# Three sets of slots for Mixer C's masked operands, half a bank per score level, and one buffer per operand part of the out-projection

## The chip, the cores and the metric

The kernel runs on one core of a Trainium2 chip. The metric is the device time of one launch in microseconds (us), and lower is better. TensorE (PE) does the matmuls, VectorE (DVE), ScalarE (ACT) and GpSimd (POOL) the element-wise work, and SyncE (SP) issues most of the DMA transfers. Each engine works through its own instructions in a fixed order and waits on semaphores for the others. Operands lie in the on-chip buffer of 128 partitions, and matmuls write to the accumulator memory, of which the program uses banks of 128 partitions x 2 KB.

## The reference

One layer of a hybrid decoder trunk, for a prompt of 2048 tokens and 64 sample tokens (8 sequences of 8) that share all weights. `x` has 1024 columns; one input projection feeds three mixers, A (gated DeltaNet), B (an RG-LRU) and C (gated linear attention, GLA), and then

```python
x = layer_norm(ALPHA * x + W_out @ [A(x) | B(x) | C(x)])
x = layer_norm(ALPHA * x + ConvFFN(x))            # d_ff = 2816

def gla_chunked(q, k, v, logf, s0):               # mixer C: 6 heads, dk 32, dv 64, chunks of 64 tokens
    # S_t = diag(f_t) S_{t-1} + k_t v_t^T ;  o_t = S_t^T q_t
```

Inside a chunk of 64 tokens, GLA needs the scores of every query with every earlier key, each weighted by the product of the per-channel forget gates between the two; between chunks a state of 32 x 64 per head is carried. Mixer C's output is normalised per head and gated before it enters `W_out`.

## The kernel before

The program has four stages, one after the other with overlaps at the seams: the input projection (to about 540 us), mixers A and B (to about 1000 us), mixer C with the out-projection and the first layer norm (`window_c`, about 985 to 1495 us), and the ConvFFN (`phase3`, to the end, almost nothing but dense matmuls). All matmuls of projections are done in three parts (`mm3`, L320): both operands are split into a high and a low part, and high x high, low x high and high x low are summed.

The change lies in `window_c`. Its work comes in nine groups: the sample group g8 (64 tokens), then g0 to g7 of 256 tokens (4 chunks). A group has 6 heads, so there are 54 heads in all.

Per group, `prep` makes decayed keys and queries (`natural`), transposes values and keys on PE (`tokens`, tiles `pv` and `pk`) and then, head by head, calls `fill` and `scores`. The scores of a chunk are found at three levels of a tree (blocks of 16, 4 and 1 tokens): level l has masked operands K1/Q1, K2/Q2, K3/Q3 of 128 x 256, and these six tiles are one set of slots. `fill` writes a head's set: ACT copies parts of K (L1347, L1355, L1358) and of Q3 (L1360, four), POOL multiplies Q1 and Q2 (L1351, six) and a row block of RC (L1361), and SP issues six DMAs K<-KN (L1349, L1357), of 32 KB each. `scores` multiplies Q by K at each level for four chunks on PE (L1373, four matmuls, eight records in the trace) and reads the result out of the accumulator into RC: ACT copies level 1 (L1376), DVE overwrites by mask with levels 2 and 3 (L1379). Masked places that nothing writes must be zero; they are cleared once, at the start, by a POOL memset of each slot tile. Two sets of slots are used in turn (`h % 2`). Levels 1 and 2 of a head share one bank (`pa`), level 3 lies in another (`pb`), and each name has one buffer per bank.

`chain` steps through a group's chunks: the state update `cs` (L1427), the output `po` (L1430), ACT's copy of the state into the next chunk's XC (L1436), and after every two chunks `head_norm` (a ones-matmul at L1206, ACT and DVE), which writes mixer C's part of `mx`.

`Project`, called P below, is the out-projection of 128 tokens `t0`: 17 calls, for the sample tokens (2048) first and then 0, 128 to 1920. `mh` is the high part of `mx` (ACT, L1524), `ml` the low part (POOL, L1525), then come two halves `pm` of 24 matmuls 128x512 each (48 a call), DVE adds the residual (L1531) and does the layer norm, SP stores `s_x1` (L1536). One call later PE transposes the result (`pt`, L1549, eight), ACT copies it into `xt` (L1550), which has a single buffer, and SP stores `s_x1T` (L1552). `pm` and `pt` share two banks. `spare()` lends the buffers of `mx`, `mh`, `ml` and `xt` to the sample group before P needs them.

The order of `window_c` on each engine is set by the scheduler of the framework, which plans with costs of its own; P is given the lowest priority, so its pieces fill places that the plan sees as free. `phase3` is scheduled by hand. A position below is told by the number of prompt score levels that stand ahead of it on PE: three for each of the 48 heads, 144 in all.

Of the kernel before, what the change touches and what calls it, by code (L numbers as in the profile page):

```python
# [9 lines left out]
F32R = mybir.dt.float32r  # L10
# [11 lines left out]
KD = DM // 128  # L22
# [281 lines left out]
def load_consts(E, pool, names):  # L304
    t = {}
    for n in names:
        o, w = _CST[n]
        t[n] = pool.tile([128, w], F32, name="c_" + n)
        E.nc.sync.dma_start(t[n], E.d["consts"][:, o:o + w])
    return t  # L310


def mm3(nc, ps, wh, wl, xh, xl, first=True, last=True, by_k=False):

    n = len(wh)
    seq = [(wh, xh), (wl, xh), (wh, xl)]
    order = [(a, k) for k in range(n) for a in range(3)] if by_k else [(a, k) for a in range(3) for k in range(n)]
    for i, (a, k) in enumerate(order):
        w, x = seq[a]
        nc.tensor.matmul(ps, w[k], x[k], start=first and i == 0, stop=last and i == 3 * n - 1)  # L320
# [854 lines left out]
def ln_scale(E, mv, m):  # L1175

    E.aset(LNEXP)
    v = mv[:m, ..., 1:2]
    E.nc.scalar.activation(v, v, AF.Ln, bias=EPS)
    E.nc.scalar.activation(v, v, AF.Exp, scale=-0.5)  # L1180
# [32 lines left out]
class Gla:  # L1213
# [4 lines left out]
    def __init__(self, E, ctx):  # L1218
        nc, tc = E.nc, E.tc
        self.E = E  # L1220
        E.aset(LNEXP)
        early = ctx.enter_context(tc.tile_pool(name="ce", bufs=1))
        self.early = ctx.enter_context(tc.tile_pool(name="cf", bufs=2))
        pool = ctx.enter_context(tc.tile_pool(name="c1", bufs=1))
        self.tr = ctx.enter_context(tc.tile_pool(name="c2", bufs=2))
        self.pg = {t: ctx.enter_context(tc.tile_pool(name="c" + t, bufs=1, space=PSUM)) for t in ("s", "tk", "g")}
        self.C = load_consts(E, early, ["m2", "m3", "m2s", "bj", "i32"])

        def ring(name, n, c, w):
            return [pool.tile([128, 6, c, w], F32, name=f"{name}{i}") for i in range(n)]  # L1230

        self.RC, self.XC, self.KC = ring("RC", 2, 4, 64), ring("XC", 2, 4, 64), ring("KC", 2, 4, 32)
        sg = [early.tile([128, 6, 1, 64], F32, name="RCs")], ring("XCs", 1, 1, 64), ring("KCs", 1, 1, 32)
        self.slots = [{n: early.tile([128, 256], F32, name=f"{n}_{i}") for n in ("K1", "Q1", "K2", "Q2", "K3", "Q3")}
                      for i in range(2)]
        self.sls = [{n: early.tile([128, 64], F32, name=f"{n}_s{i}") for n in ("K2", "Q2")} for i in range(2)]

        self.KN = [{l: early.tile([128, 512 >> t], F32, name=f"KN{l}_{t}") for l in (1, 2, 3)} for t in range(2)]

        self.DD = [{l: early.tile([128, n, 6], F32, name=f"D{l}_{i}") for l, n in ((1, 4), (2, 16), (3, 64))}  # L1240
                   for i in range(2)]
        self.ebs = pool.tile([32, 6, 8], F32, name="ebs")
        for r in sg:
            nc.vector.memset(r[0][0:64], 0.0)
        nc.vector.memset(sg[0][0][64:], 0.0)
        for d in self.sls + self.KN + self.slots:
            for w in d.values():
                nc.gpsimd.memset(w, 0.0)
        for d in self.DD:
            for w in d.values():  # L1250
                nc.gpsimd.memset(w, 1.0)
        for w in self.RC + self.XC + self.KC:
            nc.gpsimd.memset(w[0:64], 0.0)
        self.G = []
        for g in range(9):
            o = Env()
            o.g, o.smp, o.t0 = g, g == 8, g * 256
            o.RC, o.XC, o.KC = (r[0] for r in sg) if o.smp else (r[g % 2] for r in (self.RC, self.XC, self.KC))
            o.nch = 1 if o.smp else 4
            o.n = 64 * o.nch  # L1260
            self.G.append(o)
# [69 lines left out]
    def fill(self, g, h):  # L1331

        nc = self.E.nc
        t, r0 = divmod(h, 4)
        r = slice(r0 * 32, r0 * 32 + 32)
        d, n = g.nat[t], g.n
        S = self.slots[h % 2]
        if g.smp:
            sl = self.sls[h % 2]
            for a in (1, 3):  # L1340
                o = slice(32 * a, 32 * a + 32)
                nc.scalar.copy(v4(sl["K2"][o], 4)[:, :, a - 1], v4(d["k2"][r], 4)[:, :, a - 1])
                nc.gpsimd.tensor_tensor(v4(sl["Q2"][o], 4)[:, :, a], v4(d["q"][r], 4)[:, :, a],
                                        v4(d["q2"][r], 4)[:, :, a], op=OP.mult)
        for l, w in (() if g.smp else ((1, 16), (2, 4))):
            kk, qq = d[f"k{l}"][r], d[f"q{l}"][r]
            nc.scalar.copy(v4(S[f"K{l}"][32:64], w)[:, :, 0], v4(kk, w)[:, :, 0])  # L1347
            for i in range(2):
                nc.sync.dma_start(S[f"K{l}"][64 + 32 * i:96 + 32 * i, :n], self.decayed(g, t, l, i)[r])  # L1349
            for a in (1, 2, 3):  # L1350
                nc.gpsimd.tensor_tensor(v4(S[f"Q{l}"][32 * a:32 * a + 32], w)[:, :, a], v4(d["q"][r], w)[:, :, a],  # L1351
                                        v4(qq, w)[:, :, a], op=OP.mult)
        K3, Q3 = S["K3"][:, :n], S["Q3"][:, :n]
        kk, qq = d["k"][r], d["q"][r]
        nc.scalar.copy(v4(K3[0:32], 1)[:, :, 0], v4(kk, 1)[:, :, 0])  # L1355
        for i in range(2):
            nc.sync.dma_start(K3[32 + 32 * i:64 + 32 * i], self.decayed(g, t, 3, i)[r])  # L1357
        nc.scalar.copy(K3[96:128], d["k2"][r])  # L1358
        for a in range(4):
            nc.scalar.copy(v4(Q3[32 * a:32 * a + 32], 1)[:, :, a], v4(qq, 1)[:, :, a])  # L1360
        nc.gpsimd.tensor_tensor(g.RC[0:32, h].rearrange("p c i -> p (c i)"), qq, d["q0"][r], op=OP.mult)  # L1361

    def scores(self, g, h):
        nc, C, m = self.E.nc, self.C, g.nch
        o = g.RC[64:, h].rearrange("p c i -> p (c i)")
        pa = self.psum(f"s{g.g}_{h}", (128, 2, 4, 64))
        pb = self.psum(f"s3{g.g}_{h}", (128, 4, 64))
        for l in (2, 3) if g.smp else (1, 2, 3):
            ps = pb if l == 3 else pa[:, l - 1]
            K, Q = (self.sls[h % 2][x + "2"] if g.smp and l == 2 else self.slots[h % 2][f"{x}{l}"] for x in "KQ")  # L1370
            for c in range(m):
                i = slice(c * 64, (c + 1) * 64)
                nc.tensor.matmul(ps[64:, c], K[:, i], Q[:, i], start=True, stop=True)  # L1373
            a = ps[64:, :m].rearrange("p c i -> p (c i)")
            if l == 1:
                nc.scalar.copy(o, a)  # L1376
            else:
                mk = C["m2s" if g.smp and l == 2 else f"m{l}"][64:, :m * 64]
                nc.vector.copy_predicated(o, mk.bitcast(U32), a)  # L1379
# [92 lines left out]
def v4(a, w):  # L1472
    return a.rearrange("p (n a i) -> p n a i", a=4, i=w)


class Project:
# [21 lines left out]

    def spare(self):

        tags = [("mx", 2), ("mh", 2), ("ml", 2), ("xt", 1)]
        return [self.tr.tile([128, 2, 6, 64], F32, tag=t, bufs=b, name="sp" + t) for t, b in tags]

    def dest(self, t0):
# [13 lines left out]
    def __call__(self, t0):  # L1518
        E, nc = self.E, self.E.nc
        m = min(128, TT - t0)  # L1520
        mx, x = self.M[t0]
        h = self.tr.tile([128, KD, 128], F32R, tag="mh", name=f"mh{t0}")
        lo = self.tr.tile([128, KD, 128], F32R, tag="ml", name=f"ml{t0}")
        nc.scalar.copy(h, mx)  # L1524
        nc.gpsimd.tensor_tensor(lo, mx, h.bitcast(F32), op=OP.subtract)  # L1525
        for j in range(2):
            ps = self.pm.tile([128, 512], F32, tag="pm", name=f"pm{t0}{j}")
            js = slice(j * 512, (j + 1) * 512)
            mm3(nc, ps, [h[:, k] for k in range(KD)], [lo[:, k] for k in range(KD)],
                [self.wh[:, k, js] for k in range(KD)], [self.wl[:, k, js] for k in range(KD)])  # L1530
            nc.vector.scalar_tensor_tensor(x[:m, js], x[:m, js], ALPHA, ps[:m], op0=OP.mult, op1=OP.add)  # L1531
        mv = self.tr.tile([128, 2], F32, tag="mv", bufs=3, name=f"mv{t0}")
        ln_stats(E, x, m, mv, self.tr.tile([128, 2, 6], F32, tag="st", name=f"st{t0}"))
        ln_scale(E, mv, m)
        ln_apply(E, x, m, mv, self.g, self.b)
        nc.sync.dma_start(E.s["x1"][t0:t0 + m], x[:m])  # L1536
        self.done.append((t0, m, x))
# [443 lines left out]
```

## Time and profile before

| | |
|---|---|
| median of the three runs, us | 3026.18 (3017.28 to 3026.94) |
| profiled execution: time, span, us | 3025.96, 3024.2 |
| PE busy | 2886.8 us, 95% |
| DVE, ACT, POOL busy | 50%, 41%, 28% |
| first matmul of P(2048) | 1083.4 us |
| last `pm` matmul of P(1920) | begins before 1493.2 us |
| first dense run of `puv` (ConvFFN) | 1507.7 us |

The span is what the trace shows from the first to the last instruction; the execution's time is 1.8 us longer. Times below are counted from the span's start. PE is busy almost throughout, but busy is not the same as fast: the profile also gives the clock that was granted to PE (PEclk, 1.00 is full), and a matmul at half the clock is busy for longer.

### The profile page before, as it was taken

The numbers are of one execution on the slowest core, as the hardware profiler recorded it, in microseconds if no ns is written. First come the engines' busy times: TensorE is split into PE (matmuls) and PEld (weight loads), VectorE is DVE, ScalarE is ACT, GpSimd is POOL, SyncE is SP. The second block draws the span as 40 slices with busy tenths as digits, with TensorE's granted clock in tenths as the row PEclk, the third lists the DMA queues.
The fourth block names the chain that finished last, engine by engine and source line by source line (L and its number), as shares of the span: only waits on it lengthen the run. The fifth ranks groups of instructions, "written<-read, shape, count | busy, mean of one in ns | idle before, by whom it ended". The sixth has DMA issues, their size and how long they took to land.

```text
span 3024.2 us, 45238 instructions
## 1 busy us (share of the span) xinstructions
PE 2886.8 (95%) x17755; PEld 2490.4 (82%) x17755; DVE 1510.9 (50%) x2454; ACT 1231.4 (41%) x2591; POOL 844.2 (28%) x898
## 2 busy tenths in 40 slices
PE   8999999788889799999899999999999999999998
PEld 7888789777779577767678888888889999999997
DVE  4564443577663676756533333333376443344436
ACT  4474443446653687766332222222232222222223
POOL 0000001734423545444222222222232222222224
PEclk9999999789999579999899999999999999999999
DMA  6221113533433443533531111111134111111111
GB/s 198 83 74 68 58 59 96 144 101 111 114 95 99 108 130 110 150 112 117 180 116 45 46 56 49 51 48 42 49 112 146 42 52 47 48 42 42 49 43 62
DMA packets 196508, 256.77 MB, mean 85 GB/s; under 512 B 43170, under 2 KB 162040, under 8 KB 196232
## 3 DMA queue, kind: packets, MB, share of 16 engines
q1 hardware_dynamic: 194168, 246.58, 26.6%
q0 software_dynamic: 1984, 7.12, 0.6%
q8 instruction: 140, 2.29, 0.3%
q14 instruction: 72, 0.59, 0.1%
q10 hardware_dynamic: 144, 0.20, 0.0%
HBM read 183.94 MB, written 60.08 MB: 81 GB/s over the span
## 4 chain that ended last, share of the span: by engine, by line
PE 60%; DVE 4%; ACT 2%; DMA 1%; issue 1%; POOL 1%; SPq 0%; DVEq 0%; POOLq 0%; ACTq 0%
PE pug L320 16%; PE pd L320 15%; PE puv L320 15%; PE pm L320 6%; PE s L1373 2%; DVE y L1788 1%; PE pd L1870 1%; PE cs L1427 1%; ACT Q L1360 1%; PE zp L1121 1%; PE po L1206 0%; PE zp L1122 0%; PE po L1430 0%; PE zp L1123 0%; DVE act L1724 0%
## 5 line engine op out<-in xcount | busy, mean ns | idle before, releaser
L1724 DVE SCALAR_TENSOR_TENSOR act<-G,cols,act 128x1024 f32<-128x1024 f32 (+1 forms) x132 | 123.6, 950 | 492.0 <-ACT act L1722 489.6
L1877 DVE TENSOR_TENSOR y<-y,pd 128x512 f32<-128x512 f32 x322 | 220.9, 687 | 203.2 <-PE pd L320 196.7
L1615 POOL TENSOR_TENSOR wl_d<-ws_d,wh_d 128x1024 fp32r<-128x1024 f32 x44 | 106.2, 2414 | 569.9 <-ACT wh_d L1614 523.1
L320 PE MATMUL pd<-wh_d,hh 128*128 128x512 f32 x704 | 215.4, 391 | 5.6 <-DVE y L1877 3.7
L320 PE MATMUL pd<-wh_d,hl 128*128 128x512 f32 x704 | 214.9, 390 | 0.0
L320 PE MATMUL pd<-wl_d,hh 128*128 128x512 f32 x704 | 214.6, 390 | 0.0
L1704 ACT COPY G<-pug 128x512 f32<-128x512 f32 (+2 forms) x110 | 55.0, 501 | 388.2 <-PE pug L320 388.2
L320 PE MATMUL pug<-fxh,wh_g 128*128 128x512 f32 (+2 forms) x880 | 198.0, 354 | 3.3 <-ACT wh_g L1614 2.6
L320 PE MATMUL puv<-fxh,wh_v 128*128 128x512 f32 (+2 forms) x880 | 196.4, 352 | 0.8 <-ACT wh_v L1614 0.8
L320 PE MATMUL puv<-fxh,wl_v 128*128 128x512 f32 (+2 forms) x880 | 196.2, 352 | 0.2 <-POOL wl_v L1615 0.2
L320 PE MATMUL puv<-fxl,wh_v 128*128 128x512 f32 (+2 forms) x880 | 196.0, 351 | 0.0
L320 PE MATMUL pug<-fxl,wh_g 128*128 128x512 f32 (+2 forms) x880 | 196.0, 351 | 0.0
L320 PE MATMUL pug<-fxh,wl_g 128*128 128x512 f32 (+2 forms) x880 | 195.9, 351 | 0.0
L320 PE MATMUL pm<-xh,wh 128*128 128x448 f32 (+1 forms) x800 | 181.9, 360 | 7.1 <-ACT xh L370 6.3
L1614 ACT CAST wh_d<-ws_d 128x1024 fp32r<-128x1024 f32 x44 | 45.8, 1040 | 337.5 <-PE pd L1870 173.3
L320 PE MATMUL pm<-xh,wl 128*128 128x448 f32 (+1 forms) x800 | 181.6, 359 | 0.0
L320 PE MATMUL pm<-xl,wh 128*128 128x448 f32 (+1 forms) x800 | 179.8, 358 | 0.5 <-DVE xl L371 0.4
L1766 DVE TENSOR_TENSOR hl<-act,hh 128x512 fp32r<-128x512 f32 (+2 forms) x110 | 124.0, 1128 | 99.5 <-ACT hh L1758 99.5
L320 PEld LDWEIGHTS pug<-fxh,wh_g 128*128 128x128 f32 x880 | 157.0, 189 | 19.0 <-ACT wh_g L1614 3.0
L320 PEld LDWEIGHTS puv<-fxh,wh_v 128*128 128x128 f32 x880 | 156.0, 188 | 14.9 <-ACT wh_v L1614 1.2
L320 PEld LDWEIGHTS pm<-xh,wh 128*128 128x128 f32 x800 | 144.4, 188 | 28.5 <-issue 10.1
L320 PEld LDWEIGHTS puv<-fxh,wl_v 128*128 128x128 f32 x880 | 155.6, 188 | 14.3 <-POOL wl_v L1615 0.6
(731 smaller groups left out, 6273.9 us busy)
## 6 DMA issues: line engine op xcount, KB each, us to landing
ws_d<-in_w_dn SPq DMA_DIRECT2D x44, 512.0 KB
ws_g<-in_w_up SPq DMA_DIRECT2D x43, 512.0 KB
ws_v<-in_w_up SPq DMA_DIRECT2D x43, 512.0 KB
zx<-in_xT SPq DMA_DIRECT2D x56, 256.0 KB
ws<-in_w_in SPq DMA_DIRECT2D x19, 512.0 KB
K<-KN SPq DMA_DIRECT2D x288, 32.0 KB
x<-in_x SPq DMA_DIRECT2D x16, 512.0 KB
s_x<-x SPq DMA_DIRECT2D x16, 512.0 KB
```

Of the source, the lines that this page charges most:

```text
L320: nc.tensor.matmul(ps, w[k], x[k], start=first and i == 0, stop=last and i == 3 * n - 1)
L1121: nc.tensor.matmul(ps, wh[:, k], xl, start=k == 0, stop=False)
L1360: nc.scalar.copy(v4(Q3[32 * a:32 * a + 32], 1)[:, :, a], v4(qq, 1)[:, :, a])
L1373: nc.tensor.matmul(ps[64:, c], K[:, i], Q[:, i], start=True, stop=True)
L1427: nc.tensor.matmul(ps[:, h], g.KC[:, h, c], g.XC[:, h, c], start=True, stop=True)
L1614: nc.scalar.copy(h, t)
L1615: nc.gpsimd.tensor_tensor(lo, t, h.bitcast(F32), op=OP.subtract)
L1704: nc.scalar.copy(G[:, 2 + o:2 + o + m], p[:, :m])
L1724: nc.vector.scalar_tensor_tensor(dst(act), src(i), taps[i], dst(act), op0=OP.mult, op1=OP.add)
L1766: nc.vector.tensor_tensor(dst, act[:, c], hh[:, c].bitcast(F32), op=OP.subtract)
L1788: nc.vector.scalar_tensor_tensor(y[:m, js], y[:m, js], mv[:m, tt, i:i + 1], a[:m, js], op0=op, op1=OP.add if i else OP.mult)
L1877: nc.vector.tensor_tensor(y, y, ps, op=OP.add)
```

## The change

There are now three sets of slots, taken by `h % 3`. The scores no longer get tiles per head: two tiles `s0` and `s1`, of one bank each, are made once, and each level takes half of one; levels take the banks in turn. `mh` and `ml` have one buffer each instead of two. The third set adds 6 KB per partition and six POOL memsets, the single buffers free 8 KB. No other instruction is added or removed.

```diff
+        self.sb, self.ns = [self.psum(f"s{i}", (128, 2, 4, 64)) for i in range(2)], 0
...
         self.slots = [{n: early.tile([128, 256], F32, name=f"{n}_{i}") for n in ("K1", "Q1", "K2", "Q2", "K3", "Q3")}
-                      for i in range(2)]
+                      for i in range(3)]
...
-        S = self.slots[h % 2]
+        S = self.slots[h % 3]
...
-        pa = self.psum(f"s{g.g}_{h}", (128, 2, 4, 64))
-        pb = self.psum(f"s3{g.g}_{h}", (128, 4, 64))
         for l in (2, 3) if g.smp else (1, 2, 3):
-            ps = pb if l == 3 else pa[:, l - 1]
-            K, Q = (self.sls[h % 2][x + "2"] if g.smp and l == 2 else self.slots[h % 2][f"{x}{l}"] for x in "KQ")
+            ps = self.sb[self.ns % 2][:, self.ns // 2 % 2]
+            self.ns += 1
+            K, Q = (self.sls[h % 2][x + "2"] if g.smp and l == 2 else self.slots[h % 3][f"{x}{l}"] for x in "KQ")
...
-        tags = [("mx", 2), ("mh", 2), ("ml", 2), ("xt", 1)]
+        tags = [("mx", 2), ("mh", 1), ("ml", 1), ("xt", 1)]
...
-        h = self.tr.tile([128, KD, 128], F32R, tag="mh", name=f"mh{t0}")
-        lo = self.tr.tile([128, KD, 128], F32R, tag="ml", name=f"ml{t0}")
+        h = self.tr.tile([128, KD, 128], F32R, tag="mh", bufs=1, name=f"mh{t0}")
+        lo = self.tr.tile([128, KD, 128], F32R, tag="ml", bufs=1, name=f"ml{t0}")
```

The scheduler lays the rest out anew. Lines below 1227 move down by two, lines below 1364 by one. The first place is PE's queue where P(384) begins. In the names, `pm3840` is the first half of P(384), `pt1280` the first transpose tile of P(128), `Q2_1` the level-2 queries in set 1, and xN counts equal rows. Before:

```order
L320 MATMUL pm2561_11341<-wol_9781,mh256_11311 128x512
L1549 MATMUL pt1280_11378<-c_ident_9792,x128_10690 128x128 x4
L1394 MATMUL pv42_12797<-c_ident_9792,v_4_12091 64x128 x4
L1430 MATMUL po768_12435<-RC1_9696,XC1_9698 64x64
L1373 MATMUL s3_1_12266<-Q2_1_9713,K2_1_9712 64x64 x4
L1549 MATMUL pt1281_11384<-c_ident_9792,x128_10690 128x128 x4
L320 MATMUL pm3840_11395<-woh_9780,mh384_11391 128x512 x8
L320 MATMUL pm3840_11395<-woh_9780,ml384_11392 128x512 x8
L320 MATMUL pm3840_11395<-wol_9781,mh384_11391 128x512 x3
L1373 MATMUL s3_2_12304<-Q1_0_9705,K1_0_9704 64x64 x4
L1399 MATMUL pk40_12803<-c_ident_9792,kd0_4_12707 64x128
L1206 MATMUL po640_11873<-z640_11874,c_ones_9794 128x384
```

P(384) begins behind 60 of the 144 levels, with scores, transposes and norms between its matmuls. After:

```order
L1374 MATMUL s0_9685<-Q3_1_9717,K3_1_9716 64x64 x4
L1374 MATMUL s1_9686<-Q1_2_9719,K1_2_9718 64x64 x4
L1374 MATMUL s0_9685<-Q2_2_9721,K2_2_9720 64x64 x4
L1374 MATMUL s1_9686<-Q3_2_9723,K3_2_9722 64x64 x4
L1374 MATMUL s0_9685<-Q1_0_9707,K1_0_9706 64x64 x4
L1374 MATMUL s1_9686<-Q2_0_9709,K2_0_9708 64x64 x4
L320 MATMUL pm3840_11373<-woh_9794,mh384_11369 128x512 x8
L320 MATMUL pm3840_11373<-woh_9794,ml384_11370 128x512 x8
L320 MATMUL pm3840_11373<-wol_9795,mh384_11369 128x512 x8
L320 MATMUL pm3841_11399<-woh_9794,mh384_11369 128x512 x8
L320 MATMUL pm3841_11399<-woh_9794,ml384_11370 128x512 x8
L320 MATMUL pm3841_11399<-wol_9795,mh384_11369 128x512 x8
```

P(384) now begins behind 110 levels and runs through its 48 matmuls without a break. Between the last matmul of P(256), which stands behind 68 levels, and this place there is no `pm` matmul on PE, only 42 levels, 7 steps of `cs`, transposes, some `po` and one ones-matmul. The scores' rows alternate between the tiles `s0` and `s1`, where before the tiles were named by group and head.

The second place is SP's queue at the store of `xt0`, the transposed result of P(0). Before (the rows behind the store included):

```order
L1349 DMA K1_0_9704<-KN1_0_9720 32x256 x2
L1357 DMA K3_0_9708<-KN3_0_9722 32x256 x2
L1349 DMA K2_0_9706<-KN2_0_9721 32x256 x2
L1512 DMA x384_11298<-in_x 128x1024
L1349 DMA K1_1_9710<-KN1_0_9720 32x256 x2
L1552 DMA s_x1T0_73<-xt0_10849 128x8x128
L1510 DMA mx640_11904<-s_mix_71 128x5x128
L1536 DMA s_x1_72<-x128_10690 128x1024
L1349 DMA K2_1_9712<-KN2_0_9721 32x256 x2
L1357 DMA K3_1_9714<-KN3_0_9722 32x256 x2
```

Twelve K<-KN DMAs stand between the store of `xt2048` and this one. After:

```order
L1351 DMA K2_1_9714<-KN2_0_9729 32x256 x2
L1359 DMA K3_1_9716<-KN3_0_9730 32x256 x2
L1351 DMA K1_2_9718<-KN1_0_9728 32x256 x2
L1351 DMA K2_2_9720<-KN2_0_9729 32x256 x2
L1359 DMA K3_2_9722<-KN3_0_9730 32x256 x2
L1351 DMA K1_0_9706<-KN1_0_9728 32x256 x2
L1351 DMA K2_0_9708<-KN2_0_9729 32x256 x2
L1553 DMA s_x1T0_73<-xt0_10839 128x8x128
L1537 DMA s_x1_72<-x256_11230 128x1024
L1553 DMA s_x1T0_73<-xt128_11355 128x8x128
L1513 DMA x640_11872<-in_x 128x1024
L1553 DMA s_x1T0_73<-xt256_11435 128x8x128
```

The store of `xt0` has moved behind 110 K<-KN DMAs counted from the store of `xt2048`, the last of them for heads 2 and 3 of g6; the rows count pairs as x2. The stores of `xt128` and `xt256` stand right behind it.

Around these places, PE's order after is: P(2048) begins behind 26 levels (20 before); four calls (2048, 0, 128, 256) lie between the levels 26 and 68; no P between 68 and 110; then P(384), P(512) and P(640) with no score among them; four calls (768 to 1152) with the last 34 levels; and six calls (1280 to 1920 in order) with no score left. Before, eleven calls of 17 had begun by level 110, and 15 stood among the levels.

## The prediction

> **What bounds the kernel now.** I read the page first, then the busy time and clock by stage, the waits of PE and POOL, and the chain of waits at the seam to the ConvFFN. The page:
>
> ```profile
> span 3024.2 us, 45238 instructions
> PE 2886.8 (95%) x17755; PEld 2490.4 (82%) x17755; DVE 1510.9 (50%) x2454; ACT 1231.4 (41%) x2591; POOL 844.2 (28%) x898
> PEclk9999999789999579999899999999999999999999
> PE 60%; DVE 4%; ACT 2%; DMA 1%; issue 1%; POOL 1%; SPq 0%; DVEq 0%; POOLq 0%; ACTq 0%
> ```
>
> PE bounds the program as a whole, and the clock row (a digit for 75.6 us) has its lowest digit, 5, where mixer C begins. Nothing ahead of 985 us or behind the seam at about 1508 us changes, so the question is how much sooner or later PE leaves `window_c`. Busy times by stage, from a score-only stretch, then from the start of P(2048) on:
>
> ```profile
> core 0: us, PE busy (x) PEld busy (x) DVE busy (x) ACT busy (x) POOL busy (x), PEclk, DMA share, GB/s
> 1018.00:1036.00 18.00, 13.31 (x85) 8.55 (x84) 13.38 (x35) 16.17 (x52) 8.26 (x20) 0.64 0.35 86
> 1083.40:1207.60 124.20, 113.37 (x992) 88.85 (x992) 84.13 (x166) 94.41 (x273) 67.29 (x113) 0.95 0.37 104
> 1207.60:1355.00 147.40, 139.90 (x1066) 108.37 (x1067) 104.28 (x218) 105.32 (x311) 63.80 (x116) 0.97 0.47 138
> 1355.00:1453.00 98.00, 91.63 (x699) 71.57 (x698) 55.02 (x93) 55.76 (x150) 38.57 (x70) 0.97 0.37 108
> 1453.00:1493.00 40.00, 32.39 (x153) 24.08 (x151) 20.72 (x23) 14.33 (x24) 15.64 (x12) 0.83 0.52 171
> 1040.00:1080.00 40.00, 34.21 (x251) 28.04 (x249) 29.11 (x57) 22.49 (x65) 13.33 (x19) 0.50 0.61 182
> ```
>
> Where P's matmuls are mixed in, PE is 91 to 95% busy at a clock of 0.95 to 0.97. Where they are not (first and last row), ACT is 90% busy or PE runs at half its clock. So P's place among the scores matters: it fills PE while ACT, POOL and DVE make operands.
>
> Prices for PE, from the chain of waits (first three rows) and the timeline, where the start of the next group tells the pitch:
>
> ```profile
> 1482.32 11.09 PE pm L320 x48
> 1388.65 0.61 PE s L1373 x8
> 1083.41 5.49 PE pm L320 x12
> 1108.83 0.86 PE L1427 MATMUL cs<-XC,KC 128*32 128x64 f32 x12
> 1109.62 0.57 PE L1430 MATMUL po<-RC,XC 128*64 128x64 f32 x12
> 1224.56 0.60 PE L1549 MATMUL pt<-c_ident,x 128*128 128x128 f32 x4
> 1207.63 2.09 PE L320 MATMUL pm<-woh,mh 128*128 128x512 f32 x8 [0.93 <-ACT xt L1550]
> ```
>
> One P costs 11.1 us, a level 0.61, a step of `cs` 0.79 and of `po` 0.57, four transposes 0.53 to 0.60. With these and the number of rows in PE's queue, the work from P(2048)'s first matmul (1083.4) to P(1920)'s last (about 1493.2) is 17 x 11.1 + 124 x 0.61 + 32 x 0.79 + 31 x 0.57 + 31 x 0.53, and some 33 us of other small matmuls: 357 us in 410. 107 of it lie ahead of P(384)'s start (1207.6), in 124.2 us, a ratio of 1.16.
>
> **The third set of slots.** It removes the wait of `fill` for the scores two heads back.
>
> ```profile
> POOL Q L1351 <- PE s L1373: 129.8, 49, 5.9
> PE s L1373 <- POOL Q L1351: 5.8, 5, 2.8
> PE pm L320 <- ACT mh L1524: 2.4, 2, 1.8
> PE pm L320 <- ACT xt L1550: 1.5, 2, 0.9
> PE s L1373 <- ACT RC L1376: 0.7, 1, 0.7
> PE s L1373 <- DVE RC L1379: 0.8, 2, 0.5
> ```
>
> and a group of the score-only stretch:
>
> ```profile
> L1351 POOL TENSOR_TENSOR Q<-q,q 32x64 f32<-32x64 f32 x15 | 5.6, 373 | 5.2 <-PE s L1373 4.4
> ```
>
> The first fence holds waits between 1083 and 1453 us (engine, line, what it waited for; total, times, longest). POOL stood 129.8 us for a free set, but PE stood only 5.8 us for POOL's operands: POOL's wait is mostly slack. The direct gain is 0 to 5.8 us; I take 4, all in the mixed stretch at the start. The six POOL memsets go to the program's front part of the stage; POOL was 46% busy there (8.26 of 18.00), and I price them at 0; six operations of the 0.37 us of a POOL multiply (last row) bound them at 2 us.
>
> **Half a bank per level.** PE waited 0.7 + 0.8 us for read-outs in all, so at most 1.5 us is to be had. With two banks taken in turn a level still waits for the level two ahead of it, now for another reader. I take 0, with ±1.5. "PSUM — Partial Sum Buffer" of the Trainium skill (Terms, "PSUM bank") says that two engines must not be on the same bank and quadrant at once; by it half a bank is no buffer of its own, and the sum would be the same 0.
>
> **Single `mh` and `ml`.** A P's `mh` copy can start only behind the last matmul of the P before. What covers it on PE are the eight transposes and whatever scores stand between.
>
> ```profile
> L1524 ACT CAST mh<-mx 128x1024 fp32r<-128x1024 f32 x15 | 15.6, 1037 | 1.3 <-DVE mx L1210 1.1 <-PE pm L320 0.2
> L1550 ACT COPY xt<-pt 128x512 f32<-128x512 f32 x26 | 14.9, 580 | 5.1 <-PE pt L1549 4.9
> L1203 ACT ACTIVATE e<-e 128x384 f32<-128x384 f32 x15 | 7.8, 519 | 0.2
> ```
>
> 1.04 us of copy and one or two `xt` copies of 0.58 stand against two times 0.53 of transposes: 0 to 1.6 us a call, I take 0.5. Only the 9 calls with few or no scores around them pay: 4 us. The `ml` copy has the 16 high x high matmuls (3.7 us), which now stand ahead of it.
>
> **The new order, which is the main term.** Six stretches of PE's queue, against P(1920)'s last `pm` at 1493.2 before:
>
> A. P(2048) starts behind 26 levels instead of 20, and 18 more of the sample group's `ss` matmuls with them; 5.9 us of work at full clock. This stretch runs at half (0.50 in 1040 to 1080), so 5.9 x 1.78 = 10.5, and P(2048) starts at 1094. Bounds 6 and 12.
>
> B. P(2048), 0, 128 and 256 with 42 levels: 106 us of work. At the ratio 1.16 that is 123, less the 4 of the slots: 119, to 1213. Bounds 112 and 125.
>
> C. No P: 42 levels, 7.3 steps of `cs`, 3.3 of `po`, 8 transposes and small ones, 38 us at full clock. ACT was busy 94.4 + 105.3 + 55.8 = 255.5 us from 1083.4 to 1453, for 41.3 heads, 15 calls of P (1.04 + 2 x 0.58, 33 us) and 14 norms of five operations of 0.5 us (35 us); that leaves 4.5 a head, and 14 heads and one norm are 66. PE at half clock would be 38 x 1.6 = 61. In the score-only row ACT reached 16.17 of 18.00, so 66 / 0.9 = 73, which I take: to 1286. Bounds: 57 (ACT has two heads done ahead, clock stays full) and 87 (ACT no busier than the 94.41 of 124.20 of the first mixed stretch). So PE gives away about 35 us here that P's matmuls filled before.
>
> What holds P(384) back is the order: its rows stand behind 110 levels. Behind it lies `xt`'s only buffer, freed by a store on SP.
>
> ```profile
> L1349 SPq DMA_DIRECT2D K<-KN x160: 507/554/1635, 1085.1 to 1437.9; - x160
> L1552 SPq DMA_DIRECT2D s_x1T<-xt x17: 370/425/575, 1168.1 to 1510.5; - x17
> DMA to landing us min/median/max: 4.0/4.7/5.4
> ```
>
> 110 K<-KN issues of about 0.56 us ahead of that store are 62 us of SP's time alone, about as much as C lasts, so SP neither waits long nor has room. When C ends, store (4.7 us to landing), `xt128` copies and the first `pm` follow each other: I take 4 us at the start of D, as part of the issue lies under C's last scores.
>
> D. P(384), 512, 640 in a row, 40 us of work, plus 4 for that start, 3 for the half clock until PE is seen busy (P(2048) in the chain: 12 matmuls in its first 5.5 us, at half rate), and 1 of `mh`: 48, to 1334. Bounds 42 and 53.
>
> E. Four P's with the last 34 levels, 88 us of work, at the 1.05 that 147.40 by 139.90 shows in the best mixed stretch: 92, to 1426. Bounds 88 and 98.
>
> F. Six P's, no scores, 78 us of work and 3 of `mh`: 81, to 1507. Before, the same end lost time:
>
> ```profile
> 1457.54 5.36 DMA ws_g<-in_w_up
> 1464.34 1.04 ACT mh L1524
> 1467.88 2.88 DVE mx L1210
> 1494.27 6.34 DMA fxl<-s_x1T
> 1504.30 3.34 POOL wl_v L1615
> 1507.68 4.44 PE puv L320 x16
> ```
>
> In these pieces of the chain, PE waits from 1457 to 1473 for the last norm, the last `mh` and the first weights of the ConvFFN. After, the last state step stands three P's ahead, and all of this lies under dense matmuls; that gain is in F already. From the last `pm` on nothing improves: the last loads of `fxl` still wait for the end of P(1920), then `fxl` and `wl_v` on POOL, 14.5 us to `puv`. I take 0 there, between -2 and +1.
>
> The sum: 1094 + 119 + 73 + 48 + 92 + 81 = 1507 against 1493.2, +14 us. The profiled execution took 3025.96 us, 0.2 below the median, so 3040.
>
> "TensorE: Matmul & The Clock Gate" of the Trainium skill (Part 1) has it that the clock is either half or full and follows how busy PE was over some microseconds; the 0.50 of the last row by stage agrees. By that rule C would run at half clock throughout, and with PE's 61 alone for C the sum would be 1495, +2, the case of no change below.
>
> **Rivals.** Faster: C is not worth 73 us. With a third set, ACT's and POOL's operands for many heads are ready when P(256) ends, C runs at its lower bound of 57, E and F at 88 and 78, B at 114: 1094 + 114 + 57 + 46 + 88 + 78 = 1477, -16 us, or 3010. For it speak POOL's 129.8 us of waiting for slots; against it, that ACT and not POOL was 90% busy without P, and that ACT's work is unchanged. It decides when C lasts less than about 59 us with the other stretches as summed.
>
> No change: ACT runs through C without a gap (66) and the other stretches come near their lower bounds: 1094 + 116 + 66 + 46 + 91 + 80 = 1493, or 3026. The chain shows 1457 to 1473 as dead time, and a dense end wins that back; that is the case for it.
>
> Much slower: C costs 87, as state steps and scores wait on each other at half clock, and D begins with SP still behind (53): 1094 + 121 + 87 + 53 + 93 + 82 = 1530, +37, or 3063. For it speaks that SP's 62 us leave it little room; against it, that it needs both.
>
> That the change does nothing at all is excluded for the order, which has moved on every engine; for the banks it is what I expect.
>
> **Chances.** My case, +9 to +28: 0.50; much slower: 0.10; no change: 0.19; faster: 0.21. 0.3% of the time, 9 us, is about what a measurement of this kernel can tell from nothing. Slower by over 0.3% is thus 0.60, within it 0.19, faster 0.21. The range: on the low side 3012, which leaves one in ten to the faster case, on the high side 3062.
>
> **What the next profile would show.** Right: P(2048) starts near 1094; a stretch of 65 to 80 us with no `pm`, from about 1213, with PEclk well under 0.9 and ACT at 85% or more; P(384) from about 1286; no score behind about 1426; POOL's wait for slots far below 130 us. Wrong: a full clock and under 60 us in that stretch, B much shorter than 119, or bubbles of over 1 us between the dense P's.

## The result, and the profile after

The changed kernel takes 3041.32 us (median of 5 runs, 3037.89 to 3046.50) against 3026.18 before: a ratio of 1.0054, 95% interval 1.0038 to 1.0069. It is slower by 15 us, where 3040 was forecast. The profiled execution took 3038.56 us with a span of 3036.8. The page:

```profile
span 3036.8 us, 45291 instructions
PE 2885.8 (95%) x17755; PEld 2497.7 (82%) x17755; DVE 1521.1 (50%) x2454; ACT 1230.0 (41%) x2591; POOL 847.7 (28%) x904
PEclk9999999789889589799999999999999999999999
```

PE is as busy as before (2885.8 against 2886.8 us), in a span that is 12.6 us longer. In the clock row mixer C has a second low place, a 7 in the seventeenth digit (1215 to 1291 us by 75.9 us a digit), where before a 9 stood. The busy times by stage, cut near the places of the forecast (start of P(2048), 4 us behind the last matmul of P(256), then the starts of P(384), P(768) and P(1280), and the end of P(1920)):

```profile
1096.80:1218.00 121.20, 113.43 (x1029) 87.89 (x1028) 90.63 (x195) 99.30 (x305) 67.99 (x119) 0.99 0.37 103
1218.00:1290.00 72.00, 42.43 (x453) 35.37 (x450) 43.42 (x113) 58.21 (x191) 39.90 (x90) 0.72 0.31 86
1290.00:1331.70 41.70, 41.17 (x220) 33.19 (x220) 21.37 (x27) 11.77 (x25) 5.31 (x3) 0.95 0.38 115
1331.70:1422.30 90.60, 89.14 (x734) 69.12 (x733) 53.45 (x91) 56.98 (x150) 38.01 (x65) 1.00 0.40 117
1422.30:1506.50 84.20, 79.94 (x390) 64.03 (x390) 53.39 (x57) 26.88 (x52) 25.13 (x16) 0.96 0.55 177
```

Columns are the stretch, its length, busy us (and count) of PE, PE's weight loads, DVE, ACT and POOL, then the granted clock, DMA share and GB/s. The second row is the stretch without P: PE is busy 42 of 72 us, at a clock of 0.72. It falls into two parts, again as busy times:

```profile
1213.80:1278.20 64.40, 46.62 (x499) 38.79 (x497) 44.70 (x111) 56.41 (x175) 38.07 (x86) 0.78 0.28 76
1278.20:1290.00 11.80, 0.01 (x1) 0.01 (x1) 2.63 (x10) 5.63 (x26) 3.68 (x7) 0.50 0.41 126
```

While the scores run ACT is 88% busy (56.41 of 64.40), more than any other engine; then PE does nothing. How that ends is seen in the chain of waits (start, length, what; the rows at ... are further K<-KN issues) and in one row of PE's timeline:

```profile
1275.93 1.29 PE s L1374 x12
1277.63 0.58 SPq L1351
...
1285.24 0.58 SPq L1351
1285.88 3.46 DMA s_x1T<-xt
1289.35 0.59 ACT xt L1551
1289.99 6.19 PE pm L320 x18
```

```profile
1289.99 3.78 PE L320 MATMUL pm<-woh,mh 128*128 128x512 f32 x8 [11.80 <-ACT xt L1551]
```

PE has done the last score ahead of P(384) at 1278.2 and then stands 11.8 us. In the chain SP issues 13 K<-KN transfers, one after the other, for heads that PE will not reach until P(384) to P(640) are through; behind them stands the store of `xt0`, behind that the copy of `xt128`, and behind that the `pm` bank.

### The profile page after: what moved, and what is told of

It is laid out like the page before. It is cut to its first block, busy times and chain, and to the rows that moved or that the text cites. A ratio compares the mean times of both kernels' runs of the same rounds, so it can differ in the third digit from the quotient of the medians.

```text
span 3036.8 us, 45291 instructions
## 1 busy us (share of the span) xinstructions
PE 2885.8 (95%) x17755; PEld 2497.7 (82%) x17755; DVE 1521.1 (50%) x2454; ACT 1230.0 (41%) x2591; POOL 847.7 (28%) x904
## 4 chain that ended last, share of the span: by engine, by line
PE 78%; DVE 7%; ACT 6%; issue 4%; DMA 3%; POOL 2%; SPq 1%; POOLq 0%; DVEq 0%; ACTq 0%
PE pm L320 19%; PE pd L320 15%; PE pug L320 15%; PE puv L320 15%; PE s L1374 1%; PE zp L1121 1%; DVE Tm L897 1%; DVE y L1789 1%; PE zp L1122 1%; PE zp L1123 1%; ACT Q L1362 1%; ACT WU L920 1%; DVE tmp L895 1%; PE pd L1871 1%; PE cw L962 1%
## 5 line engine op out<-in xcount | busy, mean ns | idle before, releaser
L320 PEld LDWEIGHTS puv<-fxl,wh_v 128*128 128x128 f32 x880 | 156.0, 188 | 13.9
```

## The experiments

The theory to be tested: the loss is the stretch without P, and it comes with the place of the stores in SP's queue. Rival 1: the single buffers of `mh` and `ml` make bubbles, short waits of PE between calls of P. Rival 2: PE waits longer for the read-out of half banks. Each kernel was timed against the kernel before on the same chip; those medians were 3022.5 to 3024.1 us, so the ratios are to be compared, not the times.

How many prompt score levels (of 144) stand ahead of each call of P in PE's queue, in five of the kernels:

```
t0                       2048  0 128 256 384 512 640 768 896 1024 1152 1280 1408 1536 1664 1792 1920
before                     20 38  46  52  60  66  72  77  84   99  107  117  124  134  138  144  144
changed                    26 40  49  61 110 110 110 110 120  131  140  144  144  144  144  144  144
half                       20 40  50  56  67  74  83  89  96  103  110  117  127  134  144  144  144
single and half            22 40  49  59  69  80  89  97 144  144  144  144  144  144  144  144  144
changed, xt stores on ACT  26 40  49  62  72  82  91 101 107  118  125  134  142  144  144  144  144
```

**The edits one by one and in pairs.** Single buffers alone:

```diff
-        h = self.tr.tile([128, KD, 128], F32R, tag="mh", name=f"mh{t0}")
+        h = self.tr.tile([128, KD, 128], F32R, tag="mh", bufs=1, name=f"mh{t0}")
```

(likewise `ml` and `spare`).

> Only mh and ml get one buffer each; two sets of slots and the tiles of the scores as before. P(384) to P(1664) stand among the scores as before (P(384) behind 55 levels), only the last two calls have no score ahead. If the stretch without P is what costs (theory): within 6 us of before, 3020 to 3032. If the single buffers' bubbles cost (rival 1: dense calls came every 13.55 us in the changed kernel, against 12.3 us of matmuls): some of it here too, 3034 to 3042. If half a bank costs (rival 2): 3026.

Measured: 3023.94 us, ratio 1.0007 (0.9998 to 1.0016). As the theory has it; the single buffers by themselves are not the loss. Rival 1 is tested here only in part, since few calls stand without scores in this order.

Half a bank per level alone (the hunks with `self.sb`):

> Only the scores get half a bank per level, in turn; two sets of slots and two buffers of mh and ml as before. Calls of P are spread over all levels to 143, two are left at the end. Theory: within 6 us of before, 3020 to 3032. Rival 1: 3026. Rival 2 (a level waits longer for a read-out of the same bank: PE waited 8.1 us for ACT's copies in the changed kernel against 0.7): 3033 to 3042.

Measured: 2994.19 us, ratio 0.9908 (0.9894 to 0.9922). Faster by 28 us, which neither the theory nor a rival foresaw; rival 2, which had it slower, falls. The stage between 1200 and 1350 us, before and in this kernel:

```profile
1200.00:1350.00 150.00, 141.60 (x1093) 109.54 (x1092) 107.51 (x221) 110.84 (x325) 69.23 (x126) 0.97 0.44 129
```

```profile
1200.00:1350.00 150.00, 147.71 (x1180) 117.18 (x1179) 106.21 (x223) 111.28 (x329) 79.55 (x132) 0.99 0.46 136
```

PE does 1180 matmul records instead of 1093 in the same 150 us and is 98% busy. The last score starts at 1453.7 us in the kernel before and at 1419.3 here (scores from 1083 to 1453 us in this kernel):

```profile
L1374 PE MATMUL s<-Q,K x1000: 222/222/370, 1083.7 to 1419.3; 128*64 128x64 f32 x167
```

The table shows calls that lie more evenly: from P(384) to P(1408) 6 to 10 levels stand between one call and the next, where before it was 5 to 15. The kernel before has a short stretch without P of its own, a hole in the order, where the 15 stand, between P(896) and P(1024): no `pm` runs from 1302.0 to 1324.5 us. The stretch around it, before and in this kernel:

```profile
1300.00:1326.00 26.00, 19.82 (x188) 14.54 (x186) 16.13 (x34) 21.67 (x61) 17.52 (x32) 0.84 0.20 54
1300.00:1326.00 26.00, 26.00 (x196) 20.21 (x195) 23.42 (x52) 22.12 (x65) 12.90 (x20) 1.00 0.60 174
```

P(2048) starts at nearly the same time in both (1083.4 and 1084.6 us), and P(1536), behind 134 levels in both, starts at 1422.1 before and at 1400.1 here. So most of the 28 us is won among the scores, by the order. PE's waits for ACT's read-outs, which the edit touches directly, are 0.7 us before and 0.6 here.

Single buffers and half banks, two sets of slots:

> Single mh and ml and half a bank per level, two sets of slots. In the order no P stands between level 104 and level 144, and nine calls (896 to 1920) follow the last score. Theory: such a stretch of 40 levels costs here too, 70 to 80 us for about 36 us of PE's work, 3034 to 3050, though neither edit alone does. Rival 1: nine dense calls as in the changed kernel, 3036 to 3042. Rival 2: as half alone.

Measured: 3026.08 us, ratio 1.0006 (0.9997 to 1.0015). The two edits, each harmless or good alone, give away the 28 us together, with the order's hole of 40 levels. In the trace no `pm` runs from 1306.8 to 1367.9 us. It stayed below the 3034 to 3050 that were expected. The hole costs less here than in the changed kernel: 61.1 us with PE busy for 42.2 of them, at a clock of 0.84, and at its end PE waits 2.65 us for `xt` and not 11.8. Whether that accounts for all of the difference is not shown.

Three sets of slots and single buffers, score tiles as before:

> Three sets of slots and single mh and ml, tiles of the scores per head as before. Calls of P stand among the levels from 22 to 143. Theory: no stretch without P, and the waits for slots go: 3014 to 3028. Rival 1: 3034 to 3042. Rival 2: 3026 or a little less.

Measured: 3018.74 us, ratio 0.9989 (0.9980 to 0.9997). No hole as long as that, no loss; against single buffers alone (1.0007) the third set brings 5 us, within what it was priced at (0 to 5.8). The third set alone, and together with half banks alone, was not run.

**The hole taken out of the changed kernel.** All three edits stay, and only the queue of one store changes:

```diff
-            nc.sync.dma_start(E.s[f"x1T{b}"].rearrange(...)[:, :, o:o + m], xt[:, :, :m])
+            nc.scalar.dma_start(E.s[f"x1T{b}"].rearrange(...)[:, :, o:o + m], xt[:, :, :m])
```

> The changed kernel, with all three edits, but the stores of xt issued by ACT and not by SP, so that none stands behind K<-KN transfers. In the order P(384) now begins behind 72 levels, the calls are spread over the levels to 144, and three are left at the end. Theory (the loss is the stretch without P, which the place of xt0's store in SP's queue goes with): it falls from 3041 to 2988 to 3012, that is below the kernel before, since half alone, with its calls spread, came to 2994. Rival 1 (single mh and ml are the loss): 3030 to 3041, since they are kept. Rival 3 (the third set of slots, which alone among the edits was not run without the others, costs by itself): 3020 to 3035.

Measured: 3007.41 us, ratio 0.9944 (0.9931 to 0.9956). From 1.0054 to 0.9944, 33 us by seventeen stores on another queue. The planner laid the whole order out anew for it, so the 33 us are those of the new order and not of the queue alone. Where the hole was, the trace shows (busy times by stage):

```profile
1218.00:1290.00 72.00, 68.30 (x582) 53.05 (x583) 54.02 (x109) 57.88 (x172) 40.43 (x70) 1.00 0.46 140
```

PE is 68.3 us busy instead of 42.4, at full clock, with ACT as busy as in the changed kernel (57.9 against 58.2 us). Fewer scores pass in this stretch (208 records instead of 304), but 144 `pm` matmuls, the work of three calls of P, stand among them and fill what lay idle.

The same with two sets of slots:

> Single mh and ml, half a bank per level, two sets of slots, and the stores of xt issued by ACT. The calls of P are spread to level 142, three are left at the end; without the moved stores this kernel had no P between levels 104 and 144 and took 3026. Theory: 2992 to 3010. Rival 1: 3022 to 3030, no better than with the stores on SP. Against the kernel with three sets it tells what the third set is worth when no stretch is left: theory 0 to 6 us in favour of three.

Measured: 2998.49 us, ratio 0.9921 (0.9908 to 0.9935). Rival 1 falls again: single `mh` and `ml` are in this kernel. The third set, expected to gain, loses 0.0023 (the two intervals just overlap).

The store moved in the kernel with half banks alone:

> Half a bank per level alone, with the stores of xt issued by ACT; two sets of slots, two buffers of mh and ml. The order is that of half but for the last calls. Theory: 2988 to 2997, as half (2994): the queue of the store is worth nothing where it held nothing up. If ACT's issues cost by themselves: 3 to 8 us above half.

Measured: 2999.08 us, ratio 0.9922 (0.9908 to 0.9935). This is above the 2988 to 2997 of the theory, and 4 us above half by the ratios, inside the 3 to 8 us that the expectation gives for ACT's issues; but the interval overlaps with half's. So where the store held nothing up, moving it does not help, and a small price of ACT's issues is not excluded.

Is it the halves, or the banks in turn?

```diff
-            ps = self.sb[self.ns % 2][:, self.ns // 2 % 2]
+            ps = self.sb[self.ns % 2][:, 0]
```

> As half alone, but every level takes the first half of its bank, so that the halves are not used in turn, only the two banks. The order of PE is that of half. If the banks in turn and not the halves bring the gain (theory, since waits go by bank): 2991 to 2997, as half. If the second half lets a level be written while the one two ahead is read: 3005 to 3025.

Measured: 2997.84 us, ratio 0.9915 (0.9901 to 0.9928). That is 0.8 us above the range of the theory, the intervals overlap with half's, and the calls of P stand behind the same levels as in half. Splitting the bank is worth nothing that can be measured; the other parts of the edit are worth the 26 to 28 us. The reading that lies near is that levels 1 and 2 of a head no longer follow each other in one bank. But the edit also makes two tiles once where there were two per head, and no run has one without the other, so which of the two moves the planner is not shown.

**SP's queue in two other ways.** The stores of the layer norm's rows on ACT instead, those of `xt` on SP:

> The changed kernel, but the stores of the layer norm's rows s_x1 issued by ACT; those of xt stay on SP. In the order this too spreads the calls of P (P(384) behind 73 levels, none of the levels without a P for long). Theory (what matters is that SP's queue gets room and the calls stay spread, not which store it is): 3000 to 3012, as with the stores of xt on ACT (3007). If the single buffer of xt behind SP's K<-KN transfers is needed for the loss to go: 3020 to 3041.

Measured: 2999.86 us, ratio 0.9922 (0.9910 to 0.9934). Even a little better, and with `xt`'s store still behind K<-KN transfers (34 of them between the first two stores, instead of 110). So it isn't that one store: moving either kind of store off SP's queue spreads the calls of P.

A third of the K<-KN transfers on ACT:

> The changed kernel, but the two K<-KN transfers of level 3 of each head issued by ACT (one in three of them off SP), all stores on SP. The order spreads the calls to level 144, five are left at the end. Theory: most of the loss goes, 3002 to 3018; the 96 further issues and the five dense calls at the end may keep some. If the number of transfers in SP's queue has no part in it: 3036 to 3044.

Measured: 3019.21 us, ratio 0.9985 (0.9974 to 0.9995), a little above the expected range. The long hole is gone (the longest stretch without `pm` in the place where it stood is 19.7 us), but ACT now issues:

```profile
L1359 ACTq DMA_DIRECT2D K<-KN x108: 513/515/1864, 988.2 to 1368.7; - x108
```

108 issues of 0.515 us are 56 us of ACT's time in the stage where it is the busiest engine without P. That this is what keeps the kernel 12 us above the one with `xt`'s stores on ACT was not tested by itself.

What the third set costs once the hole is gone (`xt`'s stores on ACT; the sample group, g0 and g1 use two sets, the others three):

> As the changed kernel with the stores of xt issued by ACT, but the sample group, g0 and g1 take only two of the three sets of slots. P(2048) begins behind 23 levels instead of 26; the calls are spread to level 144 as before. If the third set costs only by the later start of P (theory; with three sets P(2048) started at 1097.6 us, with two at 1089.8): 2996 to 3003, against 3007 with three sets throughout and 2998 with two. If three sets cost by the order of the later groups: 3004 to 3010.

Measured: 3007.27 us, ratio 0.9946 (0.9934 to 0.9958). That theory falls. P(2048) did start earlier (1094.4 us against 1097.6), and the end did not follow. With three sets and relief by the other store the kernel took 0.9922, though there P(2048) started later still, at 1102.0. So the third set gains 5 us in one pair of kernels (next to single buffers) and loses 7 in another (with `xt`'s stores on ACT), depending on the order that comes out; which part of the order decides it stays open.

## Why the prediction was right, point by point

The kind was right: a stretch without P, in which PE gives away work time, makes the kernel slower. That the sum came out to within 1 us (1506.5 for 1507) is in part luck: A and F were 3 us too short each, B to E 0.8 to 2.3 us too long each, and inside C two errors of 8 and 9 us cancelled. The price of the half bank, wrong by 28 us, did not enter, because the new order was read and not derived from the prices.

- A: P(2048) 13.4 us later, at 1096.8; forecast 10.5, to 1094, with a bound of 12. Right in kind, 3 us short and beyond its bound. The factor 1.78 for a stretch at half clock is not worked out in the prediction; by that row's own clock and busy time (0.50, 34.21 of 40.00 us) 5.9 us of work would have been estimated at 13.8.
- B: 117 us, to P(256)'s last matmul at 1213.8; forecast 119 to 1213.
- C: forecast 73 and 4 more until P(384); measured 76.2. The parts were wrong. The scores were through after 64 us, not 73: ACT was the busiest as forecast (88%, 85% was named), but with 56.4 us of work and not 66, and the clock was 0.78 and not the half that PE's 61 us and the 1495 went by. Then PE stood 11.8 us instead of 4, because 13 transfers still stood ahead of the store when the last score ended. That SP has no room held, and I drew too small a price from it. The 62 us of its 110 issues were also set against the wrong stretch: 26 had gone out before C began, 84 fell into it, and between them SP waited, at most 4.7 us at once. That the third set is what puts the store so far back is likely but not shown: with two sets the hole ends behind the last score, where no K<-KN is left.
- D: 41.7 us from P(384)'s start, forecast 44 without the start's 4. E: 90.6, forecast 92.
- F: 84.2, forecast 81. The `mh` bubble, priced at 0.5 us a call, hardly shows: 13.6 us from call to call with one ones-matmul and a `po` step pair in it, and PE waiting 0.23 us at most ahead of a `pm`. What cost instead was one late norm at the seam. On ACT the cast of the ConvFFN's first weights (`wh_g`) stood ahead of the norm's `z` and waited 4.60 us for its load; DVE's part of the norm waited for `z`, its addition to `x` came behind that, and PE's transposes waited 3.44 us for `x`:

```profile
1459.46 1.05 ACT L1615 CAST wh_g<-ws_g 128x1024 fp32r<-128x1024 f32 x1 [4.60 <-DMA ws_g<-in_w_up]
1460.41 0.48 ACT L1207 ACTIVATE z<-po 128x384 f32<-128x384 f32 x1
1460.93 2.43 DVE L1208 SCALAR_TENSOR_TENSOR z<-e,z 128x384 f32<-128x384 f32 x1 [2.46 <-ACT z L1207]
1464.49 0.68 DVE L1532 SCALAR_TENSOR_TENSOR x<-x,pm 128x512 f32<-128x512 f32 x1
1465.22 1.12 PE L1550 MATMUL pt<-c_ident,x 128*128 128x128 f32 x4 [3.44 <-DVE x L1532]
```

```profile
1435.87 3.96 PE L320 MATMUL pm<-woh,mh 128*128 128x512 f32 x16
1449.45 3.94 PE L320 MATMUL pm<-woh,mh 128*128 128x512 f32 x16
1466.36 6.28 PE L320 MATMUL pm<-woh,mh 128*128 128x512 f32 x16
1482.27 3.93 PE L320 MATMUL pm<-woh,mh 128*128 128x512 f32 x16 [0.23 <-ACT xt L1551]
```

From one first `pm` to the next the two calls at the seam take 16.9 and 15.9 us instead of 13.6: the wait lengthens the one, and the 16 matmuls behind it, which took 6.28 us instead of 3.94 (granted clock 0.57 from 1465.2 to 1472.5 us), the other. The 3.44 us are longer than the 1 us between dense calls that the prediction named as a sign of being wrong, but they come from another cause than `mh`. From the last `pm` to `puv` 14.2 us passed (14.5 before), as forecast.

- Half a bank per level, forecast at 0 with ±1.5: wrong as a price of the edit, and the largest miss. From PE's short waits for read-outs (1.5 us) I concluded that no more was to be had. Alone the edit is worth 28 us, and by the order, which it changes far from any wait that it removes. Likely the waits were short because the order, planned around a bank that two levels share, had put other work into them; no run shows that by itself. What I had right is that a half is no buffer of its own.
- Single `mh` and `ml`, forecast 4 us: 1.0007 alone, at most 5 us by its interval. The run alone hardly tests the 4 us, since few of its calls are dense; in the changed kernel no wait of that size for `mh` shows, so F's extra time has another cause. What I did not see is that this edit, with half a bank per level, is enough for a hole.
- Third set, forecast -4: 5 us faster next to single buffers alone, no gain once the hole is gone. In the changed kernel POOL's wait for slots fell (the row is for 1097 to 1430 us), but PE's wait for POOL's operands hardly did, 5.1 us against 5.8:

```profile
POOL Q L1353 <- PE s L1374: 71.0, 29, 5.4
```

So the forecast's centre, that PE gives away work time in a stretch without P, is shown: the trace has PE busy for 46.6 of 76.2 us there, and in the order without the stretch the same three edits are 17 us faster than before and not 15 slower. "The faster rival" (C short, SP and slots no limit) did not come about in this order, and the time that it named, 3010, is close to what the same edits reach with the calls spread, by another way than the one that it named.

The best kernel of the study is half a bank per level alone, 0.9908 of the time before.

## What to carry to other kernels

Where one engine's dense work fills the gaps of a chain, price an edit by where that filler stands afterwards in the queue, before the wait that the edit removes; a short measured wait does not bound the gain of an edit when the order is planned anew with it. A planner's hole can be tested by relieving the queue that it may come from: here seventeen stores on another queue, and the order that came with it, were worth 33 us. Run edits alone and in pairs: of the three that were made together, one was worth 28 us alone, and together with the single buffers nothing was left of it.

## What the runs showed of the hardware

Issuing a DMA on ACT costs ACT about as much as it costs SP: 0.515 us at the median for K<-KN on ACT's queue, 0.542 to 0.554 on SP's. PE's granted clock was 0.78 while it ran scores without P (1213.8 to 1278.2 us of the changed kernel, PE busy for 46.62 of 64.40 us), and 1.00 where P's matmuls stood among the scores (1218 to 1290 us with `xt`'s stores on ACT, 68.30 of 72.00 us).
